# Planner costs from measured durations, and a first norm whose gain and bias stand behind the transposition

## The chip, the cores and the metric

The kernel runs on one core of one Trainium2 chip. The metric is device time in microseconds (us) of one execution: the median of three runs. Besides them one execution was recorded by the hardware profiler; every row below is from that one.

## The reference

Two layers over 256 tokens with a model width of 1024, all in float32. Cut to what matters:

```python
h = layer_norm(x, ln_in_g, ln_in_b)
for l in range(2):
    (aq, ak, av, af, bq, bc, biq, bik, biw, cq, ck, cv) = split(h @ w_in[l])
    o_a = forgetting_attention(aq, ak, av, cumsum(log_sigmoid(af + b_f)))
    o_b = top64_attention(rope(bq), latent(bc) @ w_ukv, index(rope(biq), rope(bik), biw))
    o_c = rms_norm(differential_attention(rope(cq), rope(ck), cv, lam))
    g = sigmoid(h @ w_gate[l])                      # three gates of width 1024
    merged = g_a * (o_a @ w_br_a) + g_b * (o_b @ w_br_b) + g_c * (o_c @ w_br_c)
    h = layer_norm(alpha * h + merged @ w_out[l], ln1_g[l], ln1_b[l])
    gate, val = split(h @ w_up[l])                  # d_ff 2816
    h = layer_norm(alpha * h + (silu(causal_conv3(gate)) * val) @ w_down[l], ln2_g[l], ln2_b[l])
```

A layer norm is `(h - mu) * rs * gain + bias`, with `rs = (var + eps) ** -0.5`.

## The kernel before

**Products.** A float32 matrix product is made from three fast ones. Every operand is split into a high part (ACT copies it in a rounded type) and a low part (DVE subtracts the high part from it); `mm3` issues high x high, low x high and high x low into the same PSUM bank. In the trace `hTh` and `hTl` are the two parts of the transposed activations (128 features by 256 tokens, eight such tiles), `hl` a weight tile that holds both parts, `acc` the banks of the large products, `att` the banks of transpositions and attention.

**Weights.** They stream from DRAM once, in the order of use. SP issues chunks `raw` of 512 KB (7 buffers), each chunk is split into two `hl` tiles of 128x512 (16 buffers; 332 columns in one unit). `Stream.split` issues both halves of a split, `Stream.take` hands a tile to a product, `Stream.refill` decides when the next one is split: always when fewer than `low` (3) tiles lie ready, otherwise if `hold` is off and DVE's estimated clock is less than 1 us beyond PE's.

**Order.** Nothing is scheduled at run time: each engine works through one list, and waits for semaphores. The lists are planned as the program is built. `Clocks` keeps an estimated clock for each engine; `note` adds to it what `cost` returns for an instruction, and remembers when each tile would be done. The large products are issued in straight order. All other work (rotary position, attention, norms) is written as generators, `Tasks`, of which each live one takes a step after nearly every product (`tick`). A step that needs a tile first goes through `ready(engine, tiles)`, which keeps yielding until the estimated clock has passed the tile's estimated end. So the cost table and `ready` decide between which weight splits a softmax or a norm stands on DVE.

**Stages.** Start: the first norm, on two blocks of 128 tokens (tb 0 and 1). Then for each layer the mixer (projections, with attention spread between them), gates and output product, a norm (a handover: the norm's output is transposed and split, and only then the next product can begin), the MLP, and a second handover, after which in layer 1 the final norm and the stores follow, the tail. At the start and at each handover one block's products stand beside the other block's norm: `unit_x_tbfirst` and the first part of `layer`'s MLP run all eight feature tiles of block 0, then those of block 1, and wait for the flag of each block (`ln_tail` sets it when that block's `hTh` and `hTl` have been issued).

Each instruction that goes through the planner's wrapper is recorded under one line, L242; the raw transfers are L136.

Of the kernel before, what the change touches and what calls it, by code (L numbers as in the profile page):

```python
# [51 lines left out]
BEHIND = 1000.0  # L52

# [55 lines left out]
class Stream:  # L109


    def __init__(self, nc, ve, sc, clocks, flat, raw_pool, hl_pool, plan):
# [6 lines left out]
        for (_, _, kts, cols) in plan:  # L119
            n = kts * cols  # L120
            c = len(self.chunks)
            self.chunks.append((off, n))
            off += P * n
            w = 512 if cols >= 512 else cols
            for q in range(n // w):
                self.items.append((c, q * w, w))
        self.raw, self.hl = {}, {}
# [58 lines left out]

class Clocks:
# [3 lines left out]
    def __init__(self):  # L191
        self.clk = dict(PE=0.0, DVE=0.0, ACT=0.0, POOL=0.0)
        self.done, self.read = {}, {}

    def cost(self, eng, op, out, args):
# [16 lines left out]
        return 630 if n <= 16 else 100 + 2.2 * n  # L212

    def note(self, eng, op, args, kw):
        aps = [x for x in list(args) + list(kw.values()) if isinstance(x, bass.AP)]
        if not aps:
            return
        out = aps[0]
        outs = [out.name] + ([kw["accum_out"].name] if "accum_out" in kw else [])
# [3 lines left out]
        start = max([self.clk[eng]] + [self.done.get(x.name, 0) for x in aps[1:]])  # L223
        self.clk[eng] = start + self.cost(eng, op, out, aps)
        for o in outs:
            self.done[o] = self.clk[eng] + 150
# [64 lines left out]
def tile_hybrid(ctx: ExitStack, tc: tile.TileContext, a: dict, out: bass.AP):  # L291
# [21 lines left out]
    uid = [0]  # L313

# [63 lines left out]
    lng = hp.tile([P, D], F32, name="lng0", tag="lng")  # L378
    lnb = hp.tile([P, D], F32, name="lnb0", tag="lnb")
    ident = cpool.tile([P, P], F32, name="ident")  # L380
    sc.dma_start(ident, a["cst"][:, C_ID:C_ID + P])
    sc.dma_start(posi, a["positions"].rearrange("o (t p) -> p (o t)", p=P))
    sc.dma_start(cst[:, C_INVF:], a["cst"][:, C_INVF:])
    for q in range(2):
        nc.sync.dma_start(h[0][q], xv[:, 0, 512 * q:512 * q + 512])
    for q in range(2):
        bc_load(lng[:, 512 * q:512 * q + 512], a["ln_in_g"], 512, 512 * q, nc.sync)
        bc_load(lnb[:, 512 * q:512 * q + 512], a["ln_in_b"], 512, 512 * q, nc.sync)
    W.dma()
    W.dma()  # L390
    for q in range(2):
        nc.sync.dma_start(h[1][q], xv[:, 1, 512 * q:512 * q + 512])
    nc.sync.dma_start(cst[:, C_TRI:C_INVF], a["cst"][:, C_TRI:C_INVF])
    for _ in range(RAW_BUFS - 2):
        W.dma()
# [6 lines left out]
    def small_loads():  # L402
# [3 lines left out]
        nc.sync.dma_start(convp, a["convp"])  # L406

    tri = cst[:, C_TRI:C_TRI + P]
# [25 lines left out]
    def rotary_tables():  # L434
# [16 lines left out]
        yield  # L451
# [57 lines left out]
    def store(tb, q):  # L509
        (nc.sync, sc)[q].dma_start(out[0, tb * P:(tb + 1) * P, 512 * q:512 * q + 512], h[tb][q])  # L510

    def last_norm1(st, g, b):
        mu, rs = ln_stats(st)
        for q in range(2):
            ve.scalar_tensor_tensor(h[1][q], h[1][q], mu, g[:, 512 * q:512 * q + 512], ALU.subtract, ALU.mult)
        for q in range(2):
            ve.scalar_tensor_tensor(h[1][q], h[1][q], rs, b[:, 512 * q:512 * q + 512], ALU.mult, ALU.add)
            store(1, q)

    def last_norm0(st, g, b, half_done):  # L520

        mu, rs = ln_stats(st)
        nmr = small([P, 1], "nmr")
        ve.scalar_tensor_tensor(nmr, mu, -1.0, rs, ALU.mult, ALU.mult)
        for q in range(2):
            sc.activation(h[0][q], h[0][q], AF.Identity, bias=nmr, scale=rs)
        gp.tensor_tensor(h[0][0], h[0][0], g[:, 0:512], ALU.mult)
        gp.tensor_tensor(h[0][0], h[0][0], b[:, 0:512], ALU.add)
        while not half_done:
            yield  # L530
        ve.tensor_tensor(h[0][1], h[0][1], g[:, 512:1024], ALU.mult)
        ve.tensor_tensor(h[0][1], h[0][1], b[:, 512:1024], ALU.add)
        store(0, 1)
        yield from ready("POOL", h[0][0])
        nc.sync.dma_start(out[0, 0:P, 0:512], h[0][0])
# [9 lines left out]
    def ln_tail(tb, st, hT, g, b, flag):  # L545

        ln_apply(tb, st, g, b)
# [11 lines left out]


# [12 lines left out]
    def unit_x_tbfirst(lhs, kts, ncols, ready=None):  # L573
        bk = [acc(), acc()]
        ws = []
        for tb in range(2):
            if ready is not None:
                T.until(lambda: tb in ready)
            for k in range(kts):
                if tb == 0:  # L580
                    ws.append(W.take())
                lh, ll = lhs(k, tb)
                mm3(bk[tb][:, :ncols], lh, ll, ws[k][:, 0, :ncols], ws[k][:, 1, :ncols], k == 0, k == kts - 1)
                if tb == 1:
                    W.free()
                T.tick()
# [32 lines left out]
    def layer(l, hT, hflag):  # L619
# [364 lines left out]

        if l:
            sc.preload_act_table_set("natural_log_exp_and_others")
        bk = unit_x_tbfirst(lhs, KD, 512, hflag)
        T.add(task_rope_T(evac(bk), 4, 32, 128 ** -0.5, "qbT"))
        bk = unit_x(lhs, KD, NG1)
        T.add(task_g1(evac(bk, NG1)))  # L990
# [22 lines left out]
        lng = hp.tile([P, D], F32, name=nm("lng"), tag="lng")  # L1013
        lnb = hp.tile([P, D], F32, name=nm("lnb"), tag="lnb")
        bc_load(lng, a["ln1_g"], D, l * D)
        bc_load(lnb, a["ln1_b"], D, l * D)
# [27 lines left out]
        gc = [gate(), gate()]  # L1044
        mT = [None, None]
# [34 lines left out]
        W.hold = True  # L1080
        hT1, flag1 = new_hT(), set()
        for tb in range(2):
            ts = slice(tb * P, (tb + 1) * P)
            st = small([P, 2, 6], "bst")
            for i, (nh, c0, c1) in enumerate(PIECES):
                for k in range(4):
# [7 lines left out]
                ln_half(tb, nh, st, ob[nh][tb], (c0, c1), i)  # L1094
            T.add(ln_tail(tb, st, hT1, lng, lnb, flag1))
# [11 lines left out]
        for tb in range(2):  # L1107
            T.until(lambda: tb in flag1)
            bk = acc()
            for k in range(KD):  # L1110
                if tb == 0:
                    ws.append(W.take())
                ts = slice(tb * P, (tb + 1) * P)
                mm3(bk, hT1[0][:, k, ts], hT1[1][:, k, ts], ws[k][:, 0, :], ws[k][:, 1, :], k == 0, k == KD - 1)
                if tb:
                    W.free()
                T.tick()
# [65 lines left out]
        W.hold = True  # L1183
        hT2, flag2 = new_hT(), set()
        for tb in range(2):
            ts = slice(tb * P, (tb + 1) * P)
            st = small([P, 2, 6], "bst")
            for i, (nh, c0, c1) in enumerate(PIECES):
                for d in (NPAIR - 2, NPAIR - 1):
# [9 lines left out]
                ln_half(tb, nh, st, dacc[nh][tb], (c0, c1), i)  # L1199
                if l == DEPTH - 1 and tb and nh == 0:  # L1200
                    half_done.append(1)
                    T.tick()
            if l < DEPTH - 1:
                T.add(ln_tail(tb, st, hT2, lng, lnb, flag2))
            elif tb == 0:
                half_done = []
                T.add(last_norm0(st, lng, lnb, half_done))
            else:
                last_norm1(st, lng, lnb)
        return hT2, flag2  # L1210


    hT, hflag = new_hT(), set()
# [5 lines left out]
    T.add(ln_tail(0, sts[0], hT, lng, lnb, hflag))  # L1219
# [80 lines left out]
```

## Time and profile before

| what | value |
|---|---|
| median of three runs | 935.29 us (933.64 to 935.35) |
| profiled execution: its own time | 933.45 us |
| profiled execution: span of the trace | 931.7 us |
| mean granted TensorE clock, share of full speed | 0.995 |
| PE busy | 900.1 us, 97% of the span |
| DVE busy | 655.7 us, 70% |
| ACT busy | 513.1 us, 55% |
| POOL busy | 47.0 us, 5% |

The span reaches from the first to the last instruction; 1.75 us of the execution's time lie outside it. PE is TensorE's matmuls, PEld its weight loads, DVE is VectorE, ACT ScalarE, POOL GpSimd, SP the queue that issues the weight transfers. Matmuls are pipelined, so a row of PE may overlap the one before it.

### The profile page before, as it was taken

Reading aid. Unit: us, or ns where it says so; the run is one execution under the profiler, and the core shown is the slowest. Engines: PE = TensorE matmul, PEld = TensorE weight load, DVE = VectorE, ACT = ScalarE, POOL = GpSimd, SP = SyncE. Lnnn points to the kernel's source line nnn. Section 1 sums busy time; section 2 is a strip of 40 time slices with the busy share of each in tenths; the row PEclk is TensorE's granted clock in tenths of the full one; section 3 lists DMA queues with packets and bytes.
Section 4 is the critical chain, followed back from the end, with each engine's and each line's share of the span. In section 5 each row is a group of like instructions: output and inputs, shape, how many; then the busy total and the mean of one; then the engine's idle time right before and its main releaser. Section 6 shows DMA issues by size and latency. Waiting matters only on the chain.

```text
span 931.7 us, 14406 instructions
## 1 busy us (share of the span) xinstructions
PE 900.1 (97%) x5306; PEld 787.9 (85%) x5306; DVE 655.7 (70%) x1270; ACT 513.1 (55%) x1008; POOL 47.0 (5%) x62
## 2 busy tenths in 40 slices
PE   4999999999999999999999999999999999999995
PEld 3877887888878999999888788888888799999994
DVE  7888686566678766756688957765667886766755
ACT  4753776655537655555466456765554375655540
POOL 5000010011000000000000001000110100000001
PEclk9999999999999999999999999999999999999998
DMA  8843166566526765565355322936565286566601
GB/s 307 276 141 114 48 220 236 177 200 192 189 96 227 235 196 187 181 195 182 105 185 168 113 89 72 353 115 204 186 201 176 85 295 195 178 195 188 182 3 45
DMA packets 46535, 161.45 MB, mean 173 GB/s; under 512 B 5696, under 2 KB 6208, under 8 KB 46464
## 3 DMA queue, kind: packets, MB, share of 16 engines
q1 hardware_dynamic: 44208, 154.94, 51.1%
q0 software_dynamic: 1408, 4.98, 1.6%
q8 instruction: 41, 0.67, 0.3%
q10 hardware_dynamic: 848, 0.60, 0.2%
q14 instruction: 30, 0.25, 0.1%
HBM read 159.46 MB, written 1.05 MB: 172 GB/s over the span
## 4 chain that ended last, share of the span: by engine, by line
PE 84%; DVE 9%; issue 3%; ACT 2%; DMA 1%; POOL 1%; SPq 0%; DVEq 0%; POOLq 0%; ACTq 0%
PE acc L242 52%; PE att L242 32%; DVE h L242 2%; DVE s L242 1%; DVE hl L242 1%; DVE a L242 1%; POOL rs L242 1%; DMA raw<-in_w_dram 1%; ACT a L242 1%; ACT p L242 1%; DMA lnb<-in_ln_in_b_dram 1%; DVE bst L242 1%; DVE smx L242 0%; ACT hl L242 0%; DVE t L242 0%
## 5 line engine op out<-in xcount | busy, mean ns | idle before, releaser
L242 DVE TENSOR_TENSOR hl<-raw,hl 128x512 fp32r<-128x512 f32 (+1 forms) x581 | 389.3, 695 | 185.5 <-ACT hl L242 183.9
L242 ACT ACTIVATE hl<-raw 128x512 fp32r<-128x512 f32 (+1 forms) x584 | 347.7, 624 | 192.8 <-PE att L242 92.4
L242 PE MATMUL acc<-hl,hTh 128*128 128x512 f32 (+1 forms) x896 | 285.7, 391 | 3.2 <-DVE hl L242 2.0
L242 PE MATMUL att<-hTh,hl 128*128 128x256 f32 x1280 | 231.3, 283 | 0.0
L242 PEld LDWEIGHTS att<-hTh,hl 128*128 128x128 f32 x1280 | 200.8, 192 | 1.4
L242 PEld LDWEIGHTS acc<-hl,hTh 128*128 128x128 f32 x896 | 168.3, 189 | 38.1 <-DVE hl L242 2.7
L242 PE MATMUL att<-hTl,hl 128*128 128x256 f32 x640 | 181.1, 283 | 0.0
L242 PE MATMUL acc<-hl,hTl 128*128 128x512 f32 (+1 forms) x448 | 173.4, 387 | 1.8 <-DVE hTl L242 1.8
L242 PE MATMUL acc<-hl,act 128*128 128x512 f32 x528 | 123.4, 390 | 0.0
L242 PEld LDWEIGHTS att<-hTl,hl 128*128 128x128 f32 x640 | 122.8, 192 | 0.0
L242 PEld LDWEIGHTS acc<-hl,act 128*128 128x128 f32 x528 | 97.9, 188 | 19.5
L242 PEld LDWEIGHTS acc<-hl,hTl 128*128 128x128 f32 x448 | 85.0, 190 | 17.8 <-DVE hTl L242 2.7
L242 PE MATMUL acc<-hl,oT 128*128 128x512 f32 x288 | 68.0, 391 | 0.0
L242 PEld LDWEIGHTS acc<-hl,oT 128*128 128x128 f32 x288 | 53.8, 188 | 11.0
L242 PE MATMUL acc<-hTh,hl 128*128 128x256 f32 x256 | 48.4, 289 | 3.5 <-DVE hl L242 3.5
L242 DVE SCALAR_TENSOR_TENSOR cv<-att,convp,cv 128x255 f32<-128x255 f32 x88 | 40.4, 480 | 15.4 <-ACT cv L242 13.9
L242 PE MATMUL acc<-hl,mT 128*128 128x512 f32 x192 | 45.5, 392 | 0.0
L242 PEld LDWEIGHTS acc<-hTh,hl 128*128 128x128 f32 x256 | 40.3, 192 | 5.2 <-DVE hl L242 3.9
L242 ACT ACTIVATE hTh<-att 128x512 fp32r<-128x512 f32 x16 | 9.6, 599 | 58.6 <-PE att L242 58.6
L242 PEld LDWEIGHTS acc<-hl,mT 128*128 128x128 f32 x192 | 35.6, 188 | 7.1
L242 PE MATMUL acc<-hTl,hl 128*128 128x256 f32 x128 | 36.4, 284 | 0.0
L242 POOL TENSOR_TENSOR rs<-mv,mhalf 128x1 f32<-128x1 f32 x10 | 9.1, 906 | 482.4 <-DVE mv L242 482.2
(161 smaller groups left out, 686.5 us busy)
## 6 DMA issues: line engine op xcount, KB each, us to landing
raw<-in_w_dram SPq DMA_DIRECT2D x284, 512.0 KB, 4.2
raw<-in_w_dram SPq DMA_DIRECT2D x8, 332.0 KB, 4.2
lng<-in_ln_g_dram POOLq DMA_DIRECT2D x4, 512.0 KB, 4.1
lnb<-in_ln_b_dram POOLq DMA_DIRECT2D x4, 512.0 KB, 6.4
h<-in_x_dram SPq DMA_DIRECT2D x4, 256.0 KB, 4.8
lng<-in_ln_in_g_dram SPq DMA_DIRECT2D x2, 256.0 KB, 4.9
lnb<-in_ln_in_b_dram SPq DMA_DIRECT2D x2, 256.0 KB, 5.3
wu<-in_w_ukv_dram POOLq DMA_DIRECT2D x2, 256.0 KB, 3.1
```

The source lines that it names most:

```text
L242: f(*args, **kw)
```

## The change

1. **Costs.** `Clocks.cost` gets other numbers for DVE, ACT and POOL; `note` ignores dependences within one engine, counts table loads of ACT, and keeps the high and low part of an `hl` tile apart.
2. **Gate.** `ready` also holds a step back while its engine's estimated clock is more than 2.5 us ahead of PE's, and, for DVE in the mixer, while fewer than 3 split weight tiles lie ahead.
3. **Start.** PE first runs 14 products of a constant tile whose result nobody reads (`spins`), and 9 more behind the first block's transpositions. x is loaded ahead of all else, and the gain and bias (1 MB, spread over partitions) later. The first norm only subtracts the mean and scales; gain and bias are applied per partition in PSUM behind the transposition, from a small tile `gb`. The residual copy of `h` gets its gain and bias by eight 128x512 operations in the task `first_residual`, in the gates of layer 0. The low parts of hl0 to hl3, hl6 and hl7 are made on POOL; the rotary tables follow them there. `masks` moves 24 steps into the first layer.
4. **Grouped products.** At the start and the handovers `mm3_group` runs high x high for four feature tiles, then low x high, then high x low.
5. **Handover.** `ln_apply` subtracts the mean of both halves first and then scales both. The second half of block 1's residual and statistics is moved from behind its product into `ln_tail`, after block 0's flag. `hold` is set later. A table load of ACT stands behind the block-first unit instead of ahead of it. The loads of `lng` and `lnb` of the first norm in a layer are issued after the last gate.
6. **Tail.** Both blocks of the final norm run on DVE alone, and the last stores are of 256 columns.

```diff
+LAG = 2500.0
     def cost(self, eng, op, out, args):
...
         if eng == "DVE":
-            if op == "reciprocal":
-                return 60 + 8 * n
+            if op in ("reciprocal", "bn_aggr"):
+                return 155 if op == "reciprocal" else 210
             if op == "match_replace":
-                return 140 + 1.05 * n
-            return 60 + n * (0.53 if op in ("tensor_copy", "tensor_scalar") else 1.05)
+                return 130 + 1.05 * n
+            if op == "scalar_tensor_tensor":
+                return 110 + 1.2 * n
...
+            return max(160, 125 + 0.93 * n)
...
     def ready(eng, *aps):
-        while any(clocks.done.get(x.name, 0) > clocks.now(eng) - MARGIN.get(eng, 0) for x in aps):
+
+        while (any(clocks.done.get(x.name, 0) > clocks.now(eng) - MARGIN.get(eng, 0) for x in aps)
+               or clocks.clk[eng] > clocks.clk["PE"] + LAG
+               or (eng == "DVE" and l_now[0] and W.next_split - W.used < 3)):
             yield
...
     def ln_apply(tb, st, g, b):
         mu, rs = ln_stats(st)
         for q in range(2):
-            y, gq, bq = h[tb][q], g[:, 512 * q:512 * q + 512], b[:, 512 * q:512 * q + 512]
-            ve.scalar_tensor_tensor(y, y, mu, gq, ALU.subtract, ALU.mult)
-            ve.scalar_tensor_tensor(y, y, rs, bq, ALU.mult, ALU.add)
...
-    def last_norm0(st, g, b, half_done):
...
-        gp.tensor_tensor(h[0][0], h[0][0], g[:, 0:512], ALU.mult)
-        gp.tensor_tensor(h[0][0], h[0][0], b[:, 0:512], ALU.add)
...
+        for i, (c0, c1) in enumerate(((0, 512), (512, 768), (768, 1024))):
+            y = h[tb][c0 // 512][:, c0 % 512:c0 % 512 + c1 - c0]
+            ve.scalar_tensor_tensor(y, y, rs, b[:, c0:c1], ALU.mult, ALU.add)
+            (nc.sync, sc, nc.sync)[i].dma_start(out[0, tb * P:(tb + 1) * P, c0:c1], y)
...
+    def spins(n):
+
+        for _ in range(n):
+            mm(warm, spin, spin.unsqueeze(1).broadcast_to([P, 4, P]), True)
+
+    def first_norm(tb, st, hT, flag):
+
+        mu, rs = ln_stats(st)
+        if tb:
+            yield
+        for q in range(2):
+            ve.tensor_scalar(h[tb][q], h[tb][q], mu, rs, ALU.subtract, ALU.mult)
+        yield
+        bks = []
+        for q in range(2):
+            yield from ready("PE", h[tb][q])
+            bk = yield from att()
+            bks.append(bk)
+            transpose4(bk, h[tb][q])
+            v = bk.rearrange("p (k t) -> p k t", k=4)
+            for i, f in enumerate((ALU.mult, ALU.add)):
+                ve.tensor_tensor(v, v, gb[:, i, 4 * q:4 * q + 4].unsqueeze(2).broadcast_to([P, 4, P]), f)
+        if not tb:
+            spins(9)
+            att_free(warm)
...
+    def mm3_group(o, ls, ws, first, last):
+
+        n = len(ls)
+        for i, (lh, ll) in enumerate(ls):
+            mm(o, lh, ws[i][0], first and i == 0, False)
+        T.tick()
+        for i, (lh, ll) in enumerate(ls):
+            mm(o, ll, ws[i][0], False, False)
+        T.tick()
+        for i, (lh, ll) in enumerate(ls):
+            mm(o, lh, ws[i][1], False, last and i == n - 1)
+            T.tick()
...
-                ln_half(tb, nh, st, ob[nh][tb], (c0, c1), i)
-            T.add(ln_tail(tb, st, hT1, lng, lnb, flag1))
+                if not (tb and nh):
+                    ln_half(tb, nh, st, ob[nh][tb], (c0, c1), i)
+            T.add(ln_tail(tb, st, hT1, lng, lnb, flag1, ob[1][1] if tb else None))
...
+    warm = new_bank()
+    spins(14)
...
+    for e in (ve, ve, gp, gp):
+        W.split(e)
```

Three places on DVE show how the lists move. The first is the start. Before, on DVE, block 1's norm (`h10`, `h11` are its two halves) between the weight splits:

```order
L242 TENSOR_TENSOR hl3_202<-raw1_110,hl3_202 128x512
L242 BN_STATS bst_4_150<-h10_92 128x6
L242 BN_STATS bst_4_150<-h11_93 128x6
L242 BN_AGGR mv_9_212<-bst_4_150 128x2
L242 TENSOR_SCALAR mv_9_212<-mv_9_212 128x1
L242 SCALAR_TENSOR_TENSOR h10_92<-h10_92,mv_9_212,lng0_96 128x512
L242 SCALAR_TENSOR_TENSOR h10_92<-h10_92,rs_10_215,lnb0_97 128x512
L242 SCALAR_TENSOR_TENSOR h11_93<-h11_93,mv_9_212,lng0_96 128x512
L242 SCALAR_TENSOR_TENSOR h11_93<-h11_93,rs_10_215,lnb0_97 128x512
L242 TENSOR_TENSOR hl6_226<-raw3_117,hl6_226 128x512
```

The same place now (`att_15`, `att_16` are the banks with block 1's transposed halves):

```order
L267 TENSOR_SCALAR mv_10_220<-mv_10_220 128x1
L267 TENSOR_TENSOR hl4_225<-raw2_112,hl4_225 128x512
L267 TENSOR_TENSOR hl5_228<-raw2_112,hl5_228 128x512
L267 TENSOR_SCALAR h10_92<-h10_92,mv_10_220,rs_11_223 128x512
L267 TENSOR_SCALAR h11_93<-h11_93,mv_10_220,rs_11_223 128x512
L267 TENSOR_TENSOR hl8_284<-raw4_116,hl8_284 128x332
L267 TENSOR_TENSOR hl9_291<-raw4_116,hl9_291 128x332
L267 TENSOR_TENSOR att_15_297<-att_15_297,gb_97 128x512 x2
L267 TENSOR_TENSOR att_16_304<-att_16_304,gb_97 128x512 x2
L267 TENSOR_TENSOR hTl_3_163<-att_15_297,hTh_2_162 128x4x128
L267 TENSOR_TENSOR hTl_3_163<-att_16_304,hTh_2_162 128x4x128
```

Four operations on `h` from SBUF have become two, and four in PSUM stand behind the transposition; hl6 has left DVE. The second place is DVE in the mixer of layer 0, in the softmax of the differential attention. Before:

```order
L242 TENSOR_TENSOR hl55_1253<-raw27_815,hl55_1253 128x512
L242 RECIPROCAL rina_130_1123<-ssm_150_1227 128x2
L242 TENSOR_SCALAR a1_128_1121<-a1_128_1121,rina_130_1123 128x256 x2
L242 RECIPROCAL rinv_131_1124<-ssm_152_1232 128x2
L242 TENSOR_SCALAR rinv_131_1124<-rinv_131_1124,nlam_127 128x8
L242 SCALAR_TENSOR_TENSOR a0_126_1119<-p0_127_1120,rinv_131_1124,a0_126_1119 128x128 x4
L242 SCALAR_TENSOR_TENSOR a1_128_1121<-p1_129_1122,rinv_131_1124,a1_128_1121 128x256 x4
L242 TENSOR_TENSOR hl56_1301<-raw28_883,hl56_1301 128x512
```

Now:

```order
L267 TENSOR_TENSOR hl56_1317<-raw28_975,hl56_1317 128x512
L267 RECIPROCAL rinv_127_1140<-ssm_139_1182 128x2
L267 RECIPROCAL rina_126_1139<-ssm_148_1247 128x2
L267 TENSOR_SCALAR a1_124_1137<-a1_124_1137,rina_126_1139 128x256 x2
L267 TENSOR_TENSOR hl57_1336<-raw28_975,hl57_1336 128x512
L267 RECIPROCAL rinv_127_1140<-ssm_150_1252 128x2
L267 TENSOR_SCALAR rinv_127_1140<-rinv_127_1140,nlam_125 128x8
L267 SCALAR_TENSOR_TENSOR a0_122_1135<-p0_123_1136,rinv_127_1140,a0_122_1135 128x128 x4
L267 SCALAR_TENSOR_TENSOR a1_124_1137<-p1_125_1138,rinv_127_1140,a1_124_1137 128x256 x4
L267 TENSOR_TENSOR hl58_1363<-raw29_1024,hl58_1363 128x512
```

Two weight splits (hl56, hl57) now stand ahead of the eight operations on `a0` and `a1`, which stood behind hl55. The third place is DVE at the first handover, behind the scaling of block 1's second half. Before:

```order
L242 SCALAR_TENSOR_TENSOR h11_93<-h11_93,rs_247_2756,lnb_174_1684 128x512
L242 TENSOR_TENSOR hl167_2774<-raw83_2488,hl167_2774 128x512
L242 TENSOR_TENSOR hTl_238_2667<-att_248_2782,hTh_237_2666 128x4x128
L242 TENSOR_TENSOR hl168_2789<-raw84_2521,hl168_2789 128x512
L242 TENSOR_TENSOR hTl_238_2667<-att_249_2795,hTh_237_2666 128x4x128
```

Now:

```order
L267 SCALAR_TENSOR_TENSOR h11_93<-h11_93,rs_248_2800,lnb_223_2495 128x512
L267 TENSOR_TENSOR hl168_2818<-raw84_2559,hl168_2818 128x512
L267 TENSOR_TENSOR hl169_2825<-raw84_2559,hl169_2825 128x512
L267 TENSOR_TENSOR hl170_2831<-raw85_2578,hl170_2831 128x512
L267 TENSOR_TENSOR hTl_239_2705<-att_249_2836,hTh_238_2704 128x4x128
L267 TENSOR_TENSOR hTl_239_2705<-att_250_2844,hTh_238_2704 128x4x128
```

Block 1's first low part `hTl` stood behind one weight split and stands now behind three.

## Rows read from the trace of the kernel before

**Rows 1.** The page's busy times: engine, us (share of the span) x instructions

```profile
PE 900.1 (97%) x5306; PEld 787.9 (85%) x5306; DVE 655.7 (70%) x1270; ACT 513.1 (55%) x1008; POOL 47.0 (5%) x62
```

**Rows 2.** By stretch: length, busy PE, PEld, DVE, ACT, POOL, clock, DMA share, GB/s

```profile
0.00:24.00 24.00, 11.93 (x41) 8.58 (x42) 17.24 (x31) 11.35 (x19) 13.83 (x31) 1.00 0.84 302
24.00:166.00 142.00, 138.47 (x819) 117.91 (x818) 109.22 (x290) 87.60 (x223) 5.07 (x7) 1.00 0.52 174
166.00:269.00 103.00, 103.00 (x464) 85.29 (x462) 65.83 (x94) 55.81 (x91) 5.50 (x2) 1.00 0.58 187
...
481.50:620.00 138.50, 134.95 (x799) 115.34 (x798) 103.04 (x272) 82.46 (x210) 3.93 (x5) 0.99 0.48 163
```

**Rows 3.** What PE waited for: us in total, times, longest

```profile
PE att L242 <- DMA lnb<-in_ln_in_b_dram: 8.5, 1, 8.5
PE acc L242 <- DVE hl L242: 5.4, 3, 2.0
PE att L242 <- DVE t L242: 3.0, 3, 1.4
PE acc L242 <- DVE hTl L242: 1.8, 3, 0.6
...
PE att L242 <- DVE h L242: 0.9, 4, 0.3
```

**Rows 4.** Timeline of the start: start us, duration, engine, operation

```profile
3.63 1.43 DVE L242 BATCH_NORM_STATS2 bst<-h 128x6 f32<-128x512 f32 x2 [2.62 <-DMA h<-in_x_dram]
...
5.57 0.55 POOL L242 TENSOR_TENSOR rs<-mv,mhalf 128x1 f32<-128x1 f32 x1 [5.14 <-DVE mv L242]
...
15.13 1.28 POOL L242 TENSOR_TENSOR hl<-raw,hl 128x512 fp32r<-128x512 f32 x1 [2.74 <-ACT hl L242]
...
16.73 0.63 PE L242 MATMUL acc<-hl,hTl 128*128 128x512 f32 x1
...
17.54 2.97 POOL L242 TENSOR_TENSOR hl<-raw,hl 128x512 fp32r<-128x512 f32 x2
...
17.61 1.76 DVE L242 SCALAR_TENSOR_TENSOR h<-h,rs,lnb 128x512 f32<-128x512 f32 x1 [0.47 <-POOL rs L242]
...
18.65 1.28 ACT L242 ACT_TABLE_LOAD   x1
18.72 0.40 PE L242 MATMUL acc<-hl,hTl 128*128 128x512 f32 x1
...
21.09 0.75 DVE L242 SCALAR_TENSOR_TENSOR h<-h,rs,lnb 128x512 f32<-128x512 f32 x1
...
23.98 4.26 ACT L242 ACTIVATE hl<-raw 128x332 fp32r<-128x332 f32 x10
...
31.39 0.42 DVE L242 TENSOR_TENSOR ru<-t,cc 128x256 f32<-128x256 f32 x1
...
32.25 0.42 DVE L242 TENSOR_TENSOR t<-ru,rv 128x256 f32<-128x256 f32 x1
```

**Rows 5.** The chain that ended last, to 36 us: start, duration, what

```profile
33.20 0.87 PE att L242 x8
```

**Rows 6.** Groups of DVE instructions by shape: busy us, mean ns

```profile
L242 DVE TENSOR_SCALAR p<-p,rinv 128x256 f32<-128x256 f32 x16 | 4.9, 351 | 0.3
```

**Rows 7.** Timeline of mixer 0, differential attention, DVE and PE

```profile
116.28 2.72 DVE L242 SCALAR_TENSOR_TENSOR a<-p,rinv,a 128x128 f32<-128x128 f32 x8
...
119.66 0.38 PE L242 MATMUL acc<-hTh,hl 128*128 128x256 f32 x1 [1.53 <-DVE hl L242]
```

**Rows 8.** Busy time and granted clock behind a wait in mixer 1

```profile
571.00:574.40 3.40, 3.40 (x18) 3.40 (x18) 1.92 (x4) 0.90 (x2) 0.00 (x0) 0.50 0.78 227
```

**Rows 9.** Timeline of the first handover, DVE

```profile
278.56 1.27 DVE L242 TENSOR_TENSOR hTl<-att,hTh 128x512 fp32r<-128x512 f32 x2
```

**Rows 10.** Timeline of the tail, DVE

```profile
922.01 1.63 DVE L242 TENSOR_TENSOR h<-h,lnb 128x512 f32<-128x512 f32 x1
...
926.64 1.41 DVE L242 SCALAR_TENSOR_TENSOR h<-h,rs,lnb 128x512 f32<-128x512 f32 x2
```

More of the change, by code (lines that the diff above doesn't have):

```diff
@@ L184, in refill, with part @@
             self.split(lo)
+def part(x):
+    return x.name + "low" if x.name[:2] == "hl" and x.offset % 1024 >= 512 else x.name
 class Clocks:
@@ L222, in note @@
             return
-        start = max([self.clk[eng]] + [self.done.get(x.name, 0) for x in aps[1:]])
+        start = max([self.clk[eng]] + [self.done.get(n, 0) for n in map(part, aps[1:]) if self.by.get(n) != eng])
         self.clk[eng] = start + self.cost(eng, op, out, aps)
+        if "accum_out" in kw:
+            self.clk[eng] += 155
+        if eng == "ACT" and len(args) > 2 and args[2] in TABLES and TABLES[args[2]] != self.table:
+            self.table = TABLES[args[2]]
+            self.clk[eng] += 1280
         for o in outs:
-            self.done[o] = self.clk[eng] + 150
+            self.done[o] = self.clk[eng] + (150 if eng == "PE" else 230)
+            self.by[o] = eng
         for x in aps[1:]:
@@ L313, in tile_hybrid @@
     uid = [0]
+    l_now = [0]
     def nm(s):
@@ L450, in rotary_tables @@
         gp.tensor_tensor(red, red, rn, ALU.subtract)
-        yield
+        yield from ready("ACT", red)
         sc.activation(sn16[:, :, 16:32], ang, AF.Sin)
@@ L543, in split_out, with ln_tail @@
         ve.tensor_tensor(lo, src, hi.bitcast(F32), ALU.subtract)
-    def ln_tail(tb, st, hT, g, b, flag):
+    def ln_tail(tb, st, hT, g, b, flag, bank=None):
+        if bank is not None:
+            while 0 not in flag:
+                yield
+            ln_half(tb, 1, st, bank)
         ln_apply(tb, st, g, b)
@@ L558, in ln_tail, with first_residual @@
         W.hold = len(flag) < 2
+    def spins(n):
[5 more added lines that the diff above has]
+            yield
+        for q in range(2):
+            ve.tensor_scalar(h[tb][q], h[tb][q], mu, rs, ALU.subtract, ALU.mult)
+        yield
+        bks = []
+        for q in range(2):
+            yield from ready("PE", h[tb][q])
[8 more added lines that the diff above has]
+            att_free(warm)
+        for q, bk in enumerate(bks):
+            split_out(hT[0][:, 4 * q:4 * q + 4, tb * P:(tb + 1) * P],
+                      hT[1][:, 4 * q:4 * q + 4, tb * P:(tb + 1) * P],
+                      bk.rearrange("p (k t) -> p k t", k=4))
+            att_free(bk)
+            if not tb and not q:
+                W.split(gp)
+        flag.add(tb)
+        W.hold = len(flag) < 2
+    residual = set()
+    def first_residual():
+        while not late:
+            yield
+        for tb in range(2):
+            for q in range(2):
+                y = h[tb][q]
+                for t, f in ((lng, ALU.mult), (lnb, ALU.add)):
+                    while clocks.clk["DVE"] > clocks.clk["PE"] + 300 or W.next_split - W.used < 3:
+                        yield
+                    ve.tensor_tensor(y, y, t[:, 512 * q:512 * q + 512], f)
+                    yield
+        residual.add(1)
+    late = set()
+    def mm3_group(o, ls, ws, first, last):
[9 more added lines that the diff above has]
+            T.tick()
     def unit_x(lhs, kts, ncols):
@@ L1010, in layer @@
         F["av"] = evac(unit_x(lhs, KD, 512))
[L1013 to L1016, printed above, removed]
+        l_now[0] = 0
+        late.add(1)
         mrg = [None, None]
@@ L1044, in layer @@
         gc = [gate(), gate()]
+        T.until(lambda: residual)
+        lng = hp.tile([P, D], F32, name=nm("lng"), tag="lng")
+        lnb = hp.tile([P, D], F32, name=nm("lnb"), tag="lnb")
+        bc_load(lng, a["ln1_g"], D, l * D)
+        bc_load(lnb, a["ln1_b"], D, l * D)
         mT = [None, None]
@@ L1218, in tile_hybrid @@
     W.low = -1
[L1219 removed]
+    T.add(first_norm(0, sts[0], hT, hflag))
     T.tick()
+    for _ in range(3):
+        W.split(gp)
+    T.until(lambda: 0 in hflag)
+    for q in range(2):
+        ln_half(1, q, sts[1])
+    T.add(first_norm(1, sts[1], hT, hflag))
+    T.tick()
+    for e in (ve, ve, gp, gp):
+        W.split(e)
+    T.tick()
+    W.low = LOW
     tables = rotary_tables()
     next(tables)
[L1223 to L1232 removed]
     T.add(tables)
     small_loads()
[L1235 removed]
     def task_lambdas():
[L1238 removed]
+        for _ in range(24):
+            yield
+        masks()
+        for _ in range(16):
             yield
```

125 lines of the change are left out of this document (57 added, 68 removed).

## The prediction

> **What bounds the kernel now.** I read the busy times first [rows 1]: PE works 97% of the span, so all that a change of order can win is the 3% in which PE stands, and the time in which it runs slowly. Then the table by stretch [rows 2]: in the first 24.00 us PE is busy 11.93; in mixer 0 it lacks 142.00 - 138.47 = 3.53 us, in mixer 1 138.50 - 134.95 = 3.55 us, in the gates nothing. The list of PE's waits names what it stands for [rows 3]: the load of the first norm's bias (8.5), three waits for the low part of a weight tile (5.4, of which one of 2.0 is at the start), three for a side tile t that the attention needs (3.0), and at the handovers hTl (1.8) and h (0.9). The half clock costs something too: behind a wait in mixer 1 a stretch of 3.40 us ran at a granted clock of 0.50, that is at 1.2 instead of 2.4 GHz [rows 8]; the same work at full clock takes half, so it cost 1.7 us. The end of the span is DVE's: its last scaling ends at 926.64 + 1.41 = 928.05 [rows 10].
>
> **The start.** The first point behind which the PE stream of before runs without a larger wait is the transposition of the first rotated projection, at 33.20 [rows 5]. I work out when the changed kernel can reach it, by the durations of the trace. x lands as before, the statistics run from 3.63 for 1.43, and rs is there at 5.57 + 0.55 = 6.12 [rows 4]. Then two tensor_scalar of 512 columns: at 256 columns one takes 0.351 [rows 6], so between 0.35 and 0.70; I take 0.49, since a part of such an instruction is fixed. That is 7.1. Transposed by some 7.2, the four operations in PSUM follow: the trace has no such operation on a bank in place; hTl, which reads a bank, takes 1.27 / 2 = 0.64 [rows 9], and the slowest undisturbed operation of that size near it 0.75 [rows 4]. Each waits for the one before it on the same bank, so I take 0.74 and come to 10.2; two hTl make it 11.5. Block 1: statistics 1.43, the small steps and two splits (about 0.4 and 1.3) to 14.6, two scales to 15.6, two narrow splits 0.9, four operations in PSUM 3.0, ACT's copy 0.6: 20.1. From there ACT's list decides: four copies of 332 columns at 4.26 / 10 = 0.43 [rows 4] make 1.7, a table load 1.28, the two sines some 0.5, a table load 1.28, five more copies (two narrow, three of 512 columns) about 2.5, two evacuations 1.2, together 8.5; then the rotary steps on DVE, 32.25 + 0.42 - 31.39 = 1.3 [rows 4]. That is 29.9, with some gaps 30.3, so 2.9 us earlier than 33.20.
>
> That is without disturbance. In the trace a scaling beside a subtraction on POOL took 1.76 instead of 0.75, and that subtraction 2.97 for two instead of 1.28 for one [rows 4]. The changed kernel has six splits on POOL in just this stretch, and DVE's operations from SBUF that can meet them are the four scales and the splits hl4, hl5, hl8, hl9. About three such meetings on the chain, at 1.0 us each, would leave 0.3 us of the gain. I take half of them: **1.4 us** (-0.3 to 3.0).
>
> The Trainium skill, page "SBUF — State Buffer", section "SBUF: two separate sides", says that DVE and GpSimd share one port pair, that a DVE operation with two SBUF inputs or in a two-port mode and a GpSimd operation take it in turn for a whole instruction, and that the loser blocks. By that rule every one of these meetings costs the whole remainder of POOL's instruction, and the start gains 0.3 instead of 1.4. The trace agrees as far as it goes (1.76 against 0.75); it does not show a tensor_scalar beside POOL.
>
> The 23 throwaway products cost nothing as long as PE would stand: before, it waits 8.5 us for the bias [rows 3]. The products of the start took 0.63 each until about 17 us and 0.40 from 18 us on [rows 4]; that the clock rises earlier is worth little, since ACT and DVE set 30.3. Without that cover they cost up to 23 x 0.4 = 9 us; but 14 of them stand ahead of the first transposition, which waits for h until 6.7, and 9 behind it, while block 0's hTh is made.
>
> **The mixers.** What can be had is 3.53 + 3.55 of waits [rows 2] and 1.7 of half clock [rows 8], 8.8 in all. A typical case is the one in front of mixer 0's PE at 119.66: DVE has 2.72 us of softmax steps to do at 116.28, the split that PE wants stands behind them, and PE waits 1.53 [rows 7]. In the changed list two more splits stand ahead of these steps, and no block of side work between two splits is longer than about 3 us. In the gates PE does 464 instructions in 103.00 us [rows 2], 0.222 each; a tile's six products are 1.3 us, so three tiles in hand last 4.0 and cover such a block. What could stay is a wait for t: there it is the side work itself that is late, and the new gate makes it later rather than earlier. I take **7.6** of the 8.8, one wait of 1.2 left; ends 3.0 (one wait for hl and the clock) and 8.8. DVE is busy 109.22 of 142.00 us there [rows 2], so it has room; but nothing of the work goes away.
>
> **The handovers.** Three of them, with waits of 1.8 / 3 = 0.6 for hTl and 0.9 / 3 = 0.3 for h [rows 3]. In groups of four the first hTl is wanted four products (0.9 us) later instead of one, which hides the 0.6. Block 1's norm ends a little sooner, as the scaling needn't wait between its parts; but its hTl now stands behind three splits instead of one, 1.3 us later, and needs 0.9 of that: about half a wait comes back in two of the three. I take **1.6** for the three (0 to 2.7).
>
> **The tail.** Before, DVE and POOL worked on block 0's last norm side by side, and DVE's addition there took 1.63 [rows 10], far above the usual 0.7. Now DVE does both blocks; five scalings of block 0 (some 3 us) lie before the last product's end, and the last chain ends at about 927.2 instead of 928.05; the last store is half as large. **0.8** (0.3 to 1.3).
>
> **At nothing.** The eight operations of the residual copy (8 x 0.7 = 5.6 us of DVE) lie in the gates, where DVE is busy 65.83 of 103.00 us and PE never waits [rows 2]; without this cover they would cost up to 5.6. The later loads of gain and bias (SP's and POOL's queues) land long before they are used.
>
> **Sum.** 1.4 + 7.6 + 1.6 + 0.8 = 11.4. Against the profiled execution: 933.45 - 11.4 = 922.05 us. That execution lies 1.84 below the median of the runs (935.29), and the runs are split between the two levels; the same gain from the median would be 923.9. I forecast the middle, **923.0 us**.
>
> **Rivals.**
> *The mixers give it back.* DVE does the same work; a gate that holds side work until three splits lie ahead makes the attention late, and PE waits for t instead of hl. For it speaks that 3.0 us of today's waits are for t [rows 3]; against it, that DVE has 33 us to spare in mixer 0. If all 7.6 return: 930.6 us. Chance 0.17.
> *The start collides throughout*, as worked out from the 1.76 row: gain 0.3 in place of 1.4, 924.1 us. Chance 0.15. This is what the Trainium skill's page named above says of the shared port pair.
> *All ends are good*: 3.0 + 8.8 + 2.7 + 1.3 = 15.8, so 918.6 us. Chance 0.08.
> *The change does not do what it says*: the costs only move the waits to other tiles and the start's gain is lost to POOL; within 0.2% of the median (1.9 us either way, about what a measurement of this kernel can tell): 935 us. Chance 0.06.
> *The clock falls more often.* Behind one wait of 1.93 us the clock fell, and it cost 1.7 us; today this happens once. If side work in short pieces leaves PE many short waits, each with a fall behind it, then from the ninth fall on ((935.3 + 1.9 - 923.0) / 1.7 = 8.4) the kernel is slower: 938 us or more. Against it: behind the wait of 1.53 in mixer 0 no stretch at half clock shows in that stage (1.00 in [rows 2]). Chance 0.06.
>
> **Range and chances.** The forecast's own case has 0.48, within 919.5 to 927. From 916 to 931 the range takes in the first three rivals with it, and leaves out 0.06 + 0.06 and the tails, about 0.17. Faster 0.88, same 0.06, slower 0.06.
>
> **What the profile after would show.** Right: the transposition of the first projection near 30 us; PE lacks under 2 us in the two mixers together and the granted clock stays at 1.00 behind the start; no wait for hTl of block 0; DVE's last scaling near 927 minus what was won before. Wrong: scales of 1.5 us beside POOL at the start; waits for t or hl of more than 3 us in sum in the mixers; a wait for h or hTl of block 1 of about 1 us at each handover; PE held by spins ahead of block 0's first product.

## The result, and the profile after

The changed kernel took 927.76 us (median of 4 runs, 927.42 to 927.88), the kernel before 934.46 (4 runs, 931.78 to 935.35): a ratio of 0.9934, with a 95% interval of 0.9915 to 0.9953. Forecast were 923.0 (916 to 931) and faster. So the sign and the range held, and a good half of the gain came: 6.7 us in the medians, 6.03 between the two profiled executions (933.45 and 927.42), where 11.4 had been worked out.

Where it came is read from pairs of the same instruction in both traces. The first residual sum `h<-h,acc` of each norm follows the first quarter of PE's last product ahead of that norm. Before, DVE's timeline has them at these places (start, duration):

```profile
269.43 0.69 DVE L242 SCALAR_TENSOR_TENSOR h<-h,acc 128x512 f32<-128x512 f32 x1 [2.72 <-PE acc L242]
...
459.80 0.69 DVE L242 SCALAR_TENSOR_TENSOR h<-h,acc 128x512 f32<-128x512 f32 x1 [2.15 <-PE acc L242]
...
723.35 0.69 DVE L242 SCALAR_TENSOR_TENSOR h<-h,acc 128x512 f32<-128x512 f32 x1 [2.72 <-PE acc L242]
...
913.72 0.69 DVE L242 SCALAR_TENSOR_TENSOR h<-h,acc 128x512 f32<-128x512 f32 x1 [3.10 <-PE acc L242]
```

After, with DVE's last scaling at the end:

```profile
267.86 0.69 DVE L267 SCALAR_TENSOR_TENSOR h<-h,acc 128x512 f32<-128x512 f32 x1 [1.36 <-PE acc L267]
...
457.88 0.69 DVE L267 SCALAR_TENSOR_TENSOR h<-h,acc 128x512 f32<-128x512 f32 x1 [1.36 <-PE acc L267]
...
719.08 0.69 DVE L267 SCALAR_TENSOR_TENSOR h<-h,acc 128x512 f32<-128x512 f32 x1 [1.36 <-PE acc L267]
...
909.11 0.69 DVE L267 SCALAR_TENSOR_TENSOR h<-h,acc 128x512 f32<-128x512 f32 x1 [3.10 <-PE acc L267]
...
920.76 1.53 DVE L267 SCALAR_TENSOR_TENSOR h<-h,rs,lnb 128x512 f32<-128x512 f32 x3
```

So the lead of the changed kernel is 1.57, 1.92, 4.27 and 4.61 us there. Two more points are the transposition of the first rotated projection, and in layer 1 the first 512-column product behind the narrow unit. PE's timeline has them before at

```profile
33.03 1.03 PE L242 MATMUL att<-ident,t 128*128 128x128 f32 x8
...
490.36 0.40 PE L242 MATMUL acc<-hl,hTl 128*128 128x512 f32 x1
```

and after at

```profile
31.75 1.06 PE L267 MATMUL att<-ident,t 128*128 128x128 f32 x8
...
487.55 0.39 PE L267 MATMUL acc<-hl,hTl 128*128 128x512 f32 x1
```

The leads there are 1.28 and 2.81. (The 33.20 of [rows 5] is from the chain, where a piece begins when the one before it ends; the timeline is used on both sides here.) The differences are what each part brought:

| part | forecast | measured | from |
|---|---|---|---|
| start | 1.4 | 1.3 | 33.03 - 31.75 |
| mixer 0 and gates | | 0.3 | 1.57 - 1.28 |
| handover 1 and MLP | | 0.35 | 1.92 - 1.57 |
| handover 2 | | 0.9 | 2.81 - 1.92 |
| mixer 1 and gates | | 1.5 | 4.27 - 2.81 |
| handover 3 and MLP | | 0.3 | 4.61 - 4.27 |
| three handovers | 1.6 | 1.6 | |
| two mixers | 7.6 | 1.8 | |
| tail | 0.8 | 1.4 | 6.03 - 4.61 |

The row of the start is known to about half a microsecond: the versions below with the gate of five tiles, the later place in the mixers and the handovers' hold run the same program up to this point, and stand there at 31.60, 32.26 and 32.58. Above all the mixers are off. The list of what PE waits for says with what (us in total, times, longest):

```profile
PE att L267 <- DVE t L267: 3.4, 2, 1.8
PE acc L267 <- DVE hl L267: 2.6, 3, 1.4
PE att L267 <- DVE h L267: 2.1, 3, 1.1
PE acc L267 <- ACT hTh L267: 2.1, 2, 1.4
PE att L267 <- DVE spin L267: 1.0, 1, 1.0
PE acc L267 <- DVE hTl L267: 0.9, 2, 0.5
PE acc L267 <- ACT hl L267: 0.5, 1, 0.5
PE acc L267 <- POOL hl L267: 0.4, 1, 0.4
```

Compare [rows 3]: the wait for the bias load is gone and half of those for hTl. For `h` it is 2.1 instead of 0.9, at the start. Those for t are not less (3.4 and 3.0). Of 5.4 for hl 2.6 are left, but 2.0 of the 5.4 stood at the start, so that little has gone in the mixers. By stretch, the two mixers (second and third row; the columns are those of [rows 2]):

```profile
0.00:24.00 24.00, 18.34 (x71) 10.94 (x72) 18.75 (x36) 10.77 (x20) 14.88 (x28) 0.94 0.85 282
24.00:164.40 140.40, 137.04 (x809) 116.33 (x808) 107.87 (x289) 87.71 (x220) 4.96 (x12) 1.00 0.48 166
...
479.60:615.70 136.10, 132.79 (x794) 113.14 (x792) 97.43 (x262) 77.69 (x201) 2.85 (x3) 1.00 0.42 138
```

PE lacks 3.36 and 3.31 us there, where it lacked 3.53 and 3.55 [rows 2]. So the waits account for some 0.4 of the 1.8 us. The rest is the clock: in the profiled execution of before it fell once in mixer 1 [rows 8], in this one it stays at 1.00 in both mixers. That is not clearly owed to the change. One of the experiments, with the tail alone changed, runs the program of before up to the tail; there PE waits as long in mixer 1, the clock stays up, and the tail is reached at 912.23 (line in the last section). Against that trace the changed kernel's lead is 3.12 us (912.23 - 909.11), of which start and handovers make 1.28 + 1.58 = 2.86: for the two mixers 0.3 is left. DVE and PE in mixer 0, differential attention:

```profile
116.48 0.69 DVE L267 TENSOR_TENSOR hl<-raw,hl 128x512 fp32r<-128x512 f32 x1
...
117.55 2.72 DVE L267 SCALAR_TENSOR_TENSOR a<-p,rinv,a 128x128 f32<-128x128 f32 x8
120.19 2.49 DVE L267 TENSOR_TENSOR hl<-raw,hl 128x512 fp32r<-128x512 f32 x4
...
119.25 0.28 PE L267 MATMUL acc<-hTh,hl 128*128 128x256 f32 x1
120.93 0.39 PE L267 MATMUL acc<-hTh,hl 128*128 128x256 f32 x1 [1.40 <-DVE hl L267]
```

That is the case of [rows 7] again, two weight tiles later: the eight softmax steps begin at 117.55, PE has work until 119.25 + 0.28 = 119.53, so 2.0 us in hand and not the 4.0 of three tiles, and waits until the split behind the steps is there. The same holds for t, on DVE and PE:

```profile
67.73 0.62 DVE L267 MAX8 mx<-s 128x8 f32<-128x128 f32 x2
...
70.68 0.42 DVE L267 TENSOR_TENSOR ru<-t,cc 128x256 f32<-128x256 f32 x1
...
71.54 0.42 DVE L267 TENSOR_TENSOR t<-ru,rv 128x256 f32<-128x256 f32 x1
...
72.11 0.63 PE L267 MATMUL att<-ident,t 128*128 128x128 f32 x4 [1.80 <-DVE t L267]
```

The rotary steps stand behind two rounds of the top-64 search on DVE, and PE stands at their transposition. At the start the scales of block 1 met POOL's subtractions, as in the rival on collisions. DVE, POOL, DVE, PE:

```profile
6.19 1.00 DVE L267 TENSOR_SCALAR h<-h,mv,rs 128x512 f32<-128x512 f32 x2 [0.67 <-POOL rs L267]
...
14.77 2.77 POOL L267 TENSOR_TENSOR hl<-raw,hl 128x512 fp32r<-128x512 f32 x2
14.90 2.92 DVE L267 TENSOR_SCALAR h<-h,mv,rs 128x512 f32<-128x512 f32 x2
...
20.74 1.78 PE L267 MATMUL acc<-hl,hTh 128*128 128x512 f32 x4 [1.44 <-ACT hTh L267]
```

Two scales take 1.00 us by themselves (block 0) and 2.92 beside POOL's subtractions (block 1). Behind the wait of 1.44 us in the last line PE runs at half clock for a while, which makes the 0.94 of the first 24 us in the table by stretch.

### The profile page after: what moved, and what is told of

The parts are those of the page before. It is cut to its first block, busy times and chain, and to the rows that moved or that the text cites. A ratio compares the mean times of both kernels' runs of the same rounds, so it can differ in the third digit from the quotient of the medians.

```text
span 925.6 us, 14457 instructions
## 1 busy us (share of the span) xinstructions
PE 903.9 (98%) x5329; PEld 787.8 (85%) x5329; DVE 658.6 (71%) x1283; ACT 510.4 (55%) x1006; POOL 46.4 (5%) x63
## 5 line engine op out<-in xcount | busy, mean ns | idle before, releaser
L267 PE MATMUL acc<-hl,hTh 128*128 128x512 f32 (+1 forms) x896 | 276.8, 390 | 2.5 <-ACT hTh L267 2.1
L267 PE MATMUL acc<-hl,hTl 128*128 128x512 f32 (+1 forms) x448 | 165.5, 387 | 0.9 <-DVE hTl L267 0.9
L267 ACT ACTIVATE t<-att 128x512 f32<-128x512 f32 (+1 forms) x32 | 18.2, 599 | 28.3 <-PE att L267 23.1
```

Of the source, the lines that this page charges most:

```text
L267: f(*args, **kw)
```

## The experiments

All are edits of the changed kernel unless it is said otherwise, and all compute the whole reference. The kernel before was run beside each; its medians there are 933.73 to 933.79 us (934.46 beside the changed kernel), so a difference between one of these runs and the changed kernel is good to about 0.7 us. Theory A for the mixers was that the planner's estimates run ahead of the chip, so that PE is sent to side tiles too early and the reserve of split tiles is thinner than planned. Theory B was that DVE is simply full there, and a wait taken away returns elsewhere.

**Which half of the planner pays.** The old cost table and the old way of noting when a tile is done, with the new gate (cut to one line of the table):

```diff
-            return max(160, 125 + 0.93 * n)
+            return 60 + n * (0.53 if op in ("tensor_copy", "tensor_scalar") else 1.05)
```

> The changed kernel with the old table of costs (and the old way of noting when a tile is done), but with the new gate. If the measured costs bring what the mixers gained (about 1.5 us), 929 to 930 us with the long waits of before back in the mixers; if they bring nothing and the gate does it, 927 to 928.

Measured: 924.61 us, 3.2 *faster* than with the measured costs. In the mixers there is no wait for hl any more; t costs 5.5 us in 5 waits, the longest (3.0) at the start. And the old gate, with the measured costs:

```diff
-               or clocks.clk[eng] > clocks.clk["PE"] + LAG
-               or (eng == "DVE" and l_now[0] and W.next_split - W.used < 3)):
```

> The changed kernel with the old gate (a step waits only for its tiles' estimated ends), but with the new costs. If the gate brings what the mixers gained, 929 to 931 us with a long wait for hl behind a block of softmax steps and a stretch at half clock behind it; if the costs do it, 927 to 928.

Measured: 935.41 us, no faster than the kernel before (ratio 1.0014, 1.0005 to 1.0023). The gate, both of its conditions together, is worth 7.7 us on these costs. The costs without it are a loss: start, handovers and tail bring 4.3 us by the table above, and yet the time is not below that of before. Without the gate PE waits 2.7 to 2.9 us behind the softmax steps, and the clock falls around these waits. Its waits (first row), and the granted clock (third column from the right) in mixer 0:

```profile
PE acc L267 <- DVE hl L267: 6.0, 3, 2.9
```

```profile
116.00:122.50 6.50, 3.94 (x18) 3.95 (x19) 5.00 (x11) 1.34 (x3) 0.00 (x0) 0.56 0.36 99
```

**A thicker reserve.** The gate asks for 5 split tiles in place of 3:

```diff
-               or (eng == "DVE" and l_now[0] and W.next_split - W.used < 3)):
+               or (eng == "DVE" and l_now[0] and W.next_split - W.used < 5)):
```

> The changed kernel, but DVE's side work is held back until 5 instead of 3 split weight tiles lie ahead. Theory A, the reserve of 3 is eaten by the same 2 us by which the chip lags the estimate: the waits for hl in the mixers (2.6 us, and 0.5 for ACT's part) go and the time falls by 2 to 3 us to about 925. Theory B, side work held back makes the attention late: waits for t grow by 2 us or more, 927 to 930.

Measured: 924.47 us. No wait for a split of DVE (`DVE hl`) is left in its list; t still costs 4.7 us in three waits (one of them at the start), and a wait of 0.9 for rina is new. So the reserve was too thin, and a thicker one pays. Why it was too thin is another question: theory A has the chip lag behind the plan, and for hl the plan itself says otherwise (see the part on the mixers below).

**A later place on PE's list, everywhere.**

```diff
-MARGIN = {"PE": 300.0}
+MARGIN = {"PE": 2300.0}
```

> The changed kernel, but a side step that PE needs is put on PE's list 2 us later than before against its estimated end (the margin of the gate for PE 2300 instead of 300). Theory A, the estimates run ahead of the chip by about 2 us in the mixers, so PE is sent to the rotated tile t too early: the waits for t (3.4 us) go, the time falls by 2.5 to 3.4 us to about 925. Theory B, DVE has too much to do there and a wait that is taken away returns at another tile: 927 to 928.5, with the waits for hl grown by as much as those for t shrink.

Measured: 933.31 us, 5.5 slower. The waits for t are gone and those for DVE's hl are down to 0.6, as theory A says; but this margin holds in the other stages too. At the start the transposition of the first projection stands at 35.70 instead of 31.75. In each output product PE waits for the transposed merge, and the clock falls around that wait (PE's timeline, then the window's clock, 0.66):

```profile
256.26 2.50 PE L267 MATMUL acc<-hl,mT 128*128 128x512 f32 x5 [2.35 <-DVE mT L267]
```

```profile
255.00:260.00 5.00, 3.74 (x12) 3.03 (x13) 2.50 (x4) 1.08 (x2) 0.00 (x0) 0.66 0.33 105
```

**The later place in the mixers alone.** `l_now` is set in the mixer's units:

```diff
+        extra = 2000.0 if eng == "PE" and l_now[0] else 0.0
-        while (any(clocks.done.get(x.name, 0) > clocks.now(eng) - MARGIN.get(eng, 0) for x in aps)
+        while (any(clocks.done.get(x.name, 0) > clocks.now(eng) - MARGIN.get(eng, 0) - extra for x in aps)
```

> The changed kernel with the 2 us later place on PE's list for side steps in the mixers alone (the same margin everywhere took the waits for t away, but put waits of 2.4 us for the transposed merge mT into the output products, and a later start). Theory A, PE is sent to t and to the softmax tiles too early: the two waits for t (3.4 us) go, nothing comes in the gates, 921 to 925. Theory B, the waits only move: 927 to 928.

Measured: 920.95 us, 6.8 faster than the changed kernel. PE's list of waits has no hl, and t only at the start:

```profile
PE att L267 <- DVE t L267: 1.3, 1, 1.3
PE att L267 <- ACT p L267: 1.3, 3, 0.5
```

Around the same transposition of t, DVE and PE now read:

```profile
68.72 0.42 DVE L267 TENSOR_TENSOR t<-ru,rv 128x256 f32<-128x256 f32 x1
...
70.00 1.04 PE L267 MATMUL att<-ident,t 128*128 128x128 f32 x8
```

The rotary steps end 0.86 us ahead of PE (68.72 + 0.42 against 70.00), without a wait. One thing isn't told apart by this: the later place also delays what feeds the top-64 search, so that on DVE the rotary steps now stand ahead of it. Both with 5 tiles:

> Both: side steps 2 us later on PE's list in the mixers, and side work on DVE only with 5 split tiles ahead. If the waits for hl and those for t are two causes, the gains add: 3.3 (the gate of 5 alone) and some 3, so 920.5 to 922.5, and PE waits for next to nothing in the mixers. If they share a cause, the second adds nothing: 924 to 925.

Measured: 920.92. Nothing is added, so the two edits remove the same waits for hl, and the later place those for t besides. Theory B falls: of 3.4 + 2.6 + 0.5 = 6.5 us of waits for t and hl in the mixers of the changed kernel, 1.3 for p are left with the later place, and the time is lower by as much and more. And the later place with the old costs:

> The changed kernel with the old table of costs and, in the mixers, the 2 us later place on PE's list. If the measured costs matter once PE's side steps stand late enough, the waits for t or hl come back and the time is 923 to 926; if they don't, 920.5 to 922, as with the new costs (920.95). With the old costs and without the later place it was 924.61.

Measured: 922.32 us (921.15 to 923.18), between the two answers. With PE's side steps late enough the measured costs are 1.4 better, and that need not be in the mixers: its wait for t at the start takes 3.8, with the measured costs it is 1.3.

**The meeting with POOL.**

```diff
-    for e in (ve, ve, gp, gp):
+    for e in (ve, ve, ve, ve):
```

> The changed kernel, but the low parts of hl6 and hl7 are made on DVE ahead of block 1's two scales, not on POOL beside them. By the rows of the changed kernel's start the two scales took 2.92 us beside POOL's subtractions, and 1.00 without. If the collision costs what it seems to: the scales take 1.0 again, the two splits 1.3 more of DVE, so the transposition of the first projection comes 0.6 us earlier, 927.1; if the meeting on POOL is hidden by ACT's list behind it, no change, 927.8; if DVE's list is what sets the place, 0.6 later.

Measured: 926.80 us (926.13 to 928.00). DVE's row shows the collision gone:

```profile
16.63 1.00 DVE L267 TENSOR_SCALAR h<-h,mv,rs 128x512 f32<-128x512 f32 x2
...
30.49 0.42 DVE L267 TENSOR_TENSOR t<-ru,rv 128x256 f32<-128x256 f32 x1
```

The rotated projection is ready at 30.91 instead of 31.60, 0.7 earlier (0.6 was expected); in this execution PE came to it only at 31.48, since it had waited 2.6 us for hTh and run at half clock around the end of that. So the collision costs 0.7 us, if PE is there in time; the times of the two kernels overlap (927.42 to 927.88 for the changed one).

**Without the throwaway products.**

```diff
-            spins(9)
...
-    spins(14)
```

> The changed kernel without its 23 throwaway products. Prediction's view, DVE and ACT set the start: 927.5 to 928.5, although the products of block 0 take twice as long. Rival, the clock matters: block 0's 24 products at half clock cost 24 x 0.2 = 4.8 us, of which PE's waits in the start hide about 3, so 929 to 930.

Measured: 927.89 us: nothing. Its transposition of the first projection stands at 31.86 (31.75 with them). DVE and ACT set the start, as the prediction had it.

**The handovers.** No split on demand between block 0's last tile and block 1's flag:

```diff
+                    if len(ws) == 8:
+                        W.low = -1
...
             T.until(lambda: tb in flag1)
+            W.low = LOW
```

> The changed kernel, but at the handovers no weight tile is split on demand between block 0's eighth tile and block 1's flag, so that block 1's hTl stands on DVE ahead of the three splits. The waits of 0.64 us ahead of block 1's first low product (handovers 1 and 3) go: 926.5. Rival: the three splits are late for the unit behind, and PE waits there for as long or longer: 927.8 to 929.

Measured: 926.59 us, 1.2 faster; in its list of PE's waits hTl no longer stands. The first theory held.

**The tail alone**, on the kernel before:

```diff
-                T.add(last_norm0(st, lng, lnb, half_done))
...
-                last_norm1(st, lng, lnb)
+                last_norm(tb, st, lng, lnb)
```

> The kernel before, with the final norm and the last stores of the changed kernel alone. By the two traces the way from the last statistics' input to the end of the last scaling is 1.15 us shorter, and the span's end behind it another 0.3: 932.3 us if the tail is independent of the rest; 933.7 if what it gained came from what stood ahead of it.

Measured: 932.61 us against 933.73 for the kernel before beside it, ratio 0.9986 (0.9974 to 0.9998), its runs from 930.36 to 935.01. The 1.1 fit the expectation, with an interval from 0.2 to 2.4 us. In its trace the way from the tail's first residual sum to the end of the span is 928.6 - 912.2 = 16.4 us, before 931.7 - 913.7 = 18.0.

**What paid, together**: the later place in the mixers, the handover's hold, the splits on DVE, and 6 throwaway products in the wait for hTh of block 1 (these were not tried by themselves):

```diff
-        if not tb:
-            spins(9)
+        spins(6 if tb else 9)
+        if tb:
             att_free(warm)
```

> What paid so far together: in the mixers PE's side steps 2 us later, at the handovers no splits ahead of block 1's hTl, the low parts of hl6 and hl7 on DVE, and 6 more throwaway products behind block 1's first transpositions, so that the clock does not fall in the wait for hTh. If the gains add: 920.95 - 1.2 - 0.6 to 1.0, so 918.8 to 919.2 us. If the later place on PE's list already covers the handovers, 920 to 921.

Measured: **918.19 us** (918.16 to 918.21), ratio to the kernel before 0.9834 (0.9817 to 0.9850), 9.6 us below the changed kernel and a little below the sum that was expected. PE's transposition of the first projection, and all its waits for it:

```profile
30.40 1.06 PE L267 MATMUL att<-ident,t 128*128 128x128 f32 x8 [0.44 <-DVE t L267]
```

## Why the prediction was right, and where it was wrong

**Start.** Right in its size (1.3 for 1.4) and in its parts: 1.00 for two scales (taken: 0.98), 2.77 for four operations in PSUM (taken: 2.96). Undisturbed, 30.3 was worked out for the projection; the best version, without the meeting on POOL, has 30.40. The discount is in part luck. It took half of three meetings at 1.0 us each; the trace has one, of 1.9 us on the two scales, and taking it away makes the projection ready 0.7 earlier. And three meetings would have left 2.9 - 3.0 = -0.1 of the gain, not the 0.3 that the prediction gives. The Trainium skill, page "SBUF — State Buffer", section "SBUF: two separate sides", says that GpSimd and a DVE operation in a two-port mode or with two SBUF inputs take one port pair in turn, each for a whole instruction. The trace agrees for tensor_scalar (2.92 against 1.00 us), which no row of before had shown, if that ran in such a mode; no run here shows its mode.

**Throwaway products.** Costed at nothing, and they are worth nothing (927.89 without them).

**Handovers.** The sum was right (1.6), though of the 0.9 us for `h` that it shares among them 0.34 stood at the start. The second gave 0.9: there the three splits ahead of hTl are narrow, and PE doesn't wait for it. In the first and third a wait of 0.5 us for block 1's hTl came, as expected, and the experiment that moves the splits away takes 1.2 us off.

**Tail.** Mis-sized: 1.4 for 0.8. DVE's residual sum of the last quarter no longer stands behind the addition of 1.63 us [rows 10], which ran beside one on POOL.

**Mixers.** The step that failed: "three tiles in hand last 4.0 and cover such a block". In the trace PE had 2.0 us in hand when the softmax steps began. The sum counted the three tiles from PE's place in the plan. But the new gate lets DVE's estimated clock run up to 2.5 us ahead of PE's (`LAG`), and the planner of this kernel puts these steps on DVE's list with three tiles ahead, at 115.18 us of DVE's clock and 112.94 of PE's: 2.2 of the 4.0 are gone by the plan itself, 1.8 are left, and the chip has 2.0. No run moved `LAG` by itself. For t the plan does differ from the chip: there it has t ready 0.4 us before PE comes to it, and on the chip PE waits 1.80.

The prediction read DVE's list alone. In it the two splits do stand earlier, and still the same wait came back at the next split (1.40 for 1.53). What it named as the doubt, t, stayed as it was (3.4 for 3.0). Its own signs of being wrong came true: scales of 1.5 us beside POOL, and waits for t and hl of more than 3 us in sum; PE lacks 6.67 us in the two mixers, where under 2 would have been right. The rival "the mixers give it back" was the truth for the waits: of the 7.08 us that PE lacked, 0.4 went. What came besides is the term of the clock, 1.7 in the sum and some 1.5 here, and that may be luck of the two executions that were profiled. The range held because it took in this rival. The experiments say what was lacking: with PE's side steps 2 us later in the mixers the waits go, and 6.8 us are won on top, as much as the forecast had missed and more.

**What the change's parts are worth.** "Costs as measured" is not what made it faster: with the old table it is 3.2 us faster still, without the new gate it gains nothing. The gate made good what the costs without it lose. Why the measured costs are worse with the small margin isn't settled: they move many steps at once, and no run moved single ones.

## What to carry to other kernels

In a static plan the slack between an estimate and its use on the engine that must not wait is a parameter of its own, worth more here than better costs: give it by stage, since 2 us more paid 6.8 us in the mixers and cost 12.4 us in the other stages (933.31 against 920.95), among them 3.4 at the start (35.70 against 32.26 for the first transposition) and a wait of 2.4 with a stretch at half clock in each output product. Read a moved list on both engines, the one that makes a tile and the one that waits for it; that an instruction stands earlier on the first says nothing about when it is reached. And a reserve that is counted in tiles on the plan should be compared with the trace: how long does the waiting engine run on from the moment the block begins? What one pair of traces shows as a gain may be the clock of one execution; a second trace of the same program tells.

## What the runs showed of the hardware that was not expected

The clock does not always fall behind a wait of the same length. The kernel before and the one with only the tail changed have the same program up to the tail. In the first PE waited 1.93 us in mixer 1, the granted clock fell to 0.50 [rows 8], and the twelve transpositions behind it took 2.76 us:

```profile
570.48 0.38 PE L242 MATMUL acc<-hTh,hl 128*128 128x256 f32 x1 [1.93 <-DVE hl L242]
...
571.30 2.76 PE L242 MATMUL att<-ident,a 128*128 128x128 f32 x12
```

In the second it waited as long, the clock stayed at 1.00, and they took 1.47 (PE, the window's clock, and DVE's first residual sum of the tail, 913.72 before):

```profile
570.63 0.39 PE L242 MATMUL acc<-hTh,hl 128*128 128x256 f32 x1 [1.92 <-DVE hl L242]
...
571.33 1.47 PE L242 MATMUL att<-ident,a 128*128 128x128 f32 x12
```

```profile
566.00:576.00 10.00, 8.08 (x70) 7.88 (x69) 8.09 (x20) 6.58 (x20) 0.00 (x0) 1.00 0.40 112
```

```profile
912.23 0.69 DVE L242 SCALAR_TENSOR_TENSOR h<-h,acc 128x512 f32<-128x512 f32 x1 [3.10 <-PE acc L242]
```

It comes 1.49 us earlier to the tail. The start shows the same once more. The changed kernel and the one with the gate of five tiles have the same program there, and in both PE waits 1.44 us for hTh. From 22 to 24 us the clock was 0.50 in the first and 1.00 in the second:

```profile
22.00:24.00 2.00, 2.00 (x6) 1.57 (x5) 1.95 (x5) 1.98 (x6) 1.83 (x5) 0.50 1.07 193
```

```profile
22.00:24.00 2.00, 2.00 (x9) 1.62 (x10) 2.00 (x5) 1.98 (x5) 1.69 (x5) 1.00 1.14 169
```

What decides it stays open. One fall more or less is 1.5 of the 3.6 us by which the kernel before scatters (931.78 to 935.35); that the number of falls makes the whole of it is likely and not shown. The versions in which PE never waits more than 1.8 us behind its first transposition repeat within 0.8 us, and the best within 0.05.
